# Seven half products for eight over 16 of the 22 down projection tiles of a decoder's feed-forward stage, with the residual kept in DRAM

## The chip, the cores and the metric

The kernel runs on one core of one Trainium2 chip. The metric is the time of one execution on the device in microseconds (us); each kernel is run several times and the median counts.

## The reference

One inference step of a one-layer hybrid decoder: 512 prompt tokens and 64 sample tokens (576 rows), model width 1024, feed-forward width 2816. Three recurrent branches come first and do not change here. The change lies in the last two lines:

```python
hf = rmsnorm(x, p["norm_pre_ffn"][l])
f = (jax.nn.silu(hf @ p["ffn_w_gate"][l]) * (hf @ p["ffn_w_up"][l])) @ p["ffn_w_down"][l]
x = x + rmsnorm(f, p["norm_post_ffn"][l])
```

Everything is float32.

## The kernel before

Activations lie transposed: features on the 128 partitions, tokens along the row, in two halves of NH = 288 tokens. The width 1024 is KT = 8 tiles, 2816 is FT = 22 tiles. A float32 product is made of three products of a reduced type (fp32r): each operand is split into a high part and a low remainder, and TensorE does high by high, high by low and low by high. So one 128x128 weight block against one half of the tokens is three matmuls of 128x288.

**Weights.** A load on SyncE (SP) brings a raw weight tile (`wr`) into SBUF. `wsplit` (L190) makes the high part `wh` on ScalarE (L198) and the low part `wl` = raw - high on VectorE (L199), 128x512 each. `wsplit_dma` (L178) makes the low part without VectorE: ScalarE copies the high part (L181) and its negative into the low part's buffer (L182), and a DMA issued by GpSimd (L183, a row `POOL DMA` in the trace) adds the raw weight from DRAM onto it. Buffers of `wh` and `wl` come from `ff_alloc` (L1434), which takes two pools of four in turn: a weight takes the buffer of the weight made eight before it, and its first copy waits until TensorE has read that one for the last time.

**Gate and up.** The first NG = 4 of 22 tiles are plain products. For the other 18 tiles, two at a time, `pair` (L1470) computes a 2x2 block product (two tiles of outputs by two halves of tokens) in seven half products for eight, in a Winograd form: seven weights, each against one of seven prepared activations `hx`, 12 matmuls per product, 84 instead of 96. `pair_w` (L1438) prepares the seven weights: four VectorE sums of raw quarters (L1448, L1449, L1450, L1455), four weights through `wsplit`, and three (numbers 0, 1 and 6) through `wsplit_dma`. Its work is issued under `tc.high_priority`, so the scheduler, which writes out the order of every engine's queue when the kernel is built, puts it between the products of the tiles ahead. Products run in the order 0, 2, 3, 4, 1, 5, 6, and VectorE combines them from PSUM by adds of 128x288.

**Down.** After the gate pair of every second step, `down(k0, 4)` (L1499) multiplies four finished tiles of the gated activations (`fh`, `fl`, made by `act_split`) by the down weights: for eight output tiles and two halves a full product of 12 matmuls each, 192 per chunk; weights through `wsplit` alone; the result is added to `mx` by VectorE (L1515), 16 adds of 128x288 per chunk. This is done for K tiles 0 to 15 in four chunks; `down(16, 2)` adds two more, and the last chunk of four tiles (L1541 on) is done half by half with the square, the norm and the output behind it. `mx` is the buffer `xr`; the residual `x1` stays in SBUF throughout.

## Time and profile before

| | us |
|---|---|
| median of 3 runs | 1097.94 (1096.48 to 1100.03) |
| the profiled execution, own time | 1097.48 |
| its span in the profile | 1095.6 |
| PE busy (7658 records) | 1036.4 (95%) |
| PEld busy | 989.7 (90%) |
| DVE busy | 779.4 (71%) |
| ACT busy | 508.2 (46%) |
| POOL busy | 164.4 (15%) |
| TensorE clock, mean over the span | 0.97 |
| the stage of feed-forward pairs and down chunks | about 705 to 1077 |

Busy is the union of an engine's instructions. PE is TensorE's matmuls, PEld its weight loads (one ahead of each matmul, beside the one before), DVE is VectorE, ACT ScalarE, POOL GpSimd; SPq is SyncE's queue of DMA issues. The reader should take the busy shares by stage, since the stages ahead of 705 us do not change.

### The profile page before, as it was taken

The numbers are of one execution on the slowest core, as the hardware profiler recorded it, in microseconds if no ns is written. First come the engines' busy times: TensorE is split into PE (matmuls) and PEld (weight loads), VectorE is DVE, ScalarE is ACT, GpSimd is POOL, SyncE is SP. The second block draws the span as 40 slices with busy tenths as digits, with TensorE's granted clock in tenths as the row PEclk, the third lists the DMA queues.
The fourth block names the chain that finished last, engine by engine and source line by source line (L and its number), as shares of the span: only waits on it lengthen the run. The fifth ranks groups of instructions, "written<-read, shape, count | busy, mean of one in ns | idle before, by whom it ended". The sixth has DMA issues, their size and how long they took to land.

```text
span 1095.6 us, 20107 instructions
## 1 busy us (share of the span) xinstructions
PE 1036.4 (95%) x7658; PEld 989.7 (90%) x7658; DVE 779.4 (71%) x1893; ACT 508.2 (46%) x1041; POOL 164.4 (15%) x224
## 2 busy tenths in 40 slices
PE   8889997799999999999799999899999999999994
PEld 6788896799999989998699999899999999999994
DVE  7978878737897769854637647874685766757756
ACT  5359667336444523332233445354653635635620
POOL 1132311110001210011000031200211201112124
PEclk9989997799999999999799999999999999999997
DMA  6656753373323134222112622134573736646502
GB/s 210 170 118 134 167 112 94 74 177 106 111 81 93 49 118 138 68 71 97 39 54 69 240 78 76 41 92 129 121 197 72 174 107 137 180 96 143 156 1 86
DMA packets 75139, 122.58 MB, mean 112 GB/s; under 512 B 28187, under 2 KB 36643, under 8 KB 75043
## 3 DMA queue, kind: packets, MB, share of 16 engines
q1 hardware_dynamic: 61938, 97.44, 27.6%
q0 software_dynamic: 13104, 23.86, 13.2%
q8 instruction: 60, 0.98, 0.4%
q14 instruction: 37, 0.30, 0.1%
HBM read 113.03 MB, written 8.24 MB: 111 GB/s over the span
## 4 chain that ended last, share of the span: by engine, by line
PE 74%; DVE 9%; DMA 7%; ACT 5%; issue 4%; POOL 1%; SPq 0%; DVEq 0%; POOLq 0%; ACTq 0%
PE mm L216 12%; PE mm L217 12%; PE mm L218 12%; PE mm L1466 9%; PE mm L1464 9%; PE mm L1465 9%; DMA wl<-in_w_in 1%; DVE wl L199 1%; DMA wl<-in_w_up 1%; ACT wh L181 1%; PE kp L1032 1%; DMA wr<-in_w_in 1%; DMA ys<-s5y 1%; PE zq L1203 1%; DMA wr<-in_w_gate 1%
## 5 line engine op out<-in xcount | busy, mean ns | idle before, releaser
L218 PE MATMUL mm<-hh,wl 128*128 128x288 f32 x768 | 231.3, 303 | 5.5 <-DMA wl<-in_w_in 5.5
L216 PE MATMUL mm<-hh,wh 128*128 128x288 f32 x768 | 231.4, 303 | 4.7 <-DVE u L412 2.4
L217 PE MATMUL mm<-hl,wh 128*128 128x288 f32 x768 | 231.6, 302 | 0.0
L198 ACT ACTIVATE wh<-wr 128x512 fp32r<-128x512 f32 x213 | 131.9, 629 | 212.4 <-PE mm L217 117.5
L199 DVE TENSOR_TENSOR wl<-wr,wh 128x512 fp32r<-128x512 f32 x213 | 146.8, 696 | 67.4 <-ACT wh L198 61.9
L216 PEld LDWEIGHTS mm<-hh,wh 128*128 128x128 f32 x768 | 145.8, 190 | 10.8 <-issue 5.8
L218 PEld LDWEIGHTS mm<-hh,wl 128*128 128x128 f32 x768 | 146.1, 191 | 8.6 <-DMA wl<-in_w_in 6.5
L217 PEld LDWEIGHTS mm<-hl,wh 128*128 128x128 f32 x768 | 146.1, 190 | 3.3 <-issue 2.9
L1466 PE MATMUL mm<-fh,wl 128*128 128x288 f32 x352 | 103.8, 295 | 0.0
L1464 PE MATMUL mm<-fh,wh 128*128 128x288 f32 x320 | 94.7, 296 | 0.0
L1465 PE MATMUL mm<-fl,wh 128*128 128x288 f32 x320 | 94.3, 295 | 0.0
L181 ACT ACTIVATE wh<-wr 128x512 fp32r<-128x512 f32 x91 | 56.8, 627 | 64.5 <-PE mm L1465 46.5
L1466 PE MATMUL mm<-hfh,wl 128*128 128x288 f32 x288 | 84.7, 296 | 1.0 <-DMA wl<-in_w_gate 0.8
L1465 PE MATMUL mm<-hfl,wh 128*128 128x288 f32 x288 | 84.9, 295 | 0.0
L1464 PE MATMUL mm<-hfh,wh 128*128 128x288 f32 x288 | 84.8, 295 | 0.0
L216 PE MATMUL mm<-brh,wh 128*128 128x288 f32 x224 | 67.4, 307 | 5.8 <-ACT brh L253 4.2
L217 PE MATMUL mm<-brl,wh 128*128 128x288 f32 x224 | 68.2, 306 | 0.2 <-DVE brl L254 0.2
L218 PE MATMUL mm<-brh,wl 128*128 128x288 f32 x224 | 67.5, 302 | 0.0
L1466 PEld LDWEIGHTS mm<-fh,wl 128*128 128x128 f32 x352 | 66.1, 188 | 0.0
L1465 PE MATMUL mm<-t,wh 128*128 128x288 f32 x216 | 63.9, 296 | 0.0
L1466 PE MATMUL mm<-t,wl 128*128 128x288 f32 x216 | 63.8, 295 | 0.0
L1464 PE MATMUL mm<-t,wh 128*128 128x288 f32 x216 | 63.7, 295 | 0.0
(506 smaller groups left out, 2580.8 us busy)
## 6 DMA issues: line engine op xcount, KB each, us to landing
wr<-in_w_in SPq DMA_DIRECT2D x48, 512.0 KB, 3.5
wr<-in_w_gate SPq DMA_DIRECT2D x22, 512.0 KB, 3.5
wr<-in_w_up SPq DMA_DIRECT2D x22, 512.0 KB, 3.5
wr<-in_w_down SPq DMA_DIRECT2D x20, 512.0 KB, 4.8
wl<-in_w_in POOLq DMA_DIRECT2D x30, 256.0 KB, 5.9
wl<-in_w_gate POOLq DMA_DIRECT2D x27, 256.0 KB, 4.5
wl<-in_w_up POOLq DMA_DIRECT2D x27, 256.0 KB, 4.4
wr<-in_w_out SPq DMA_DIRECT2D x8, 512.0 KB, 3.5
```

Of the source, the lines that this page charges most:

```text
L181: S.activation(hi, raw, AF.Copy)
L198: S.activation(hi, raw, AF.Copy)
L199: (eng or lo_eng()).tensor_tensor(lo, raw, hi.bitcast(F32), op=OP.subtract)
L216: PE.matmul(acc, hi[:, k, :], xh[:, sl], start=k0 + k == 0, stop=False)
L217: PE.matmul(acc, hi[:, k, :], xl[:, sl], start=False, stop=False)
L218: PE.matmul(acc, lo[:, k, :], xh[:, sl], start=False, stop=k0 + k == n - 1)
L1032: PE.matmul(kp[:, b], k2[:, sl], kqe[:, :, sl], start=True, stop=True)
L1203: PE.matmul(zqv[:, b], s0[:, b, :], kqe[:, :, c0:c0 + 8], start=True, stop=True)
L1464: PE.matmul(acc, hi[:, k0 + k, :], xh, start=new and k == 0, stop=False, skip_group_check=not new)
L1465: PE.matmul(acc, hi[:, k0 + k, :], xl, start=False, stop=False, skip_group_check=not new)
L1466: PE.matmul(acc, lo[:, k0 + k, :], xh, start=False, stop=k == len(x) - 1, skip_group_check=not new)
```

## The change

The down projection of K tiles 0 to 15 takes the same form as gate and up. Per chunk of four K tiles, `down7(k0)` treats four output pairs (two groups `g` by two pairs `e`) as 2x2 block products with two K tiles per side: seven half products of 6 matmuls per output pair, 168 per chunk. Two calls of `pair_w` per chunk make its weights, and each weight serves two output pairs, `e` = 0 and 1; so each chunk has 14 prepared weights, six of them through `wsplit_dma`. The activations need seven sides, made by `down_x0` and `down_x1`: four VectorE sums and seven splits of 128x2x288 per chunk. `down7` now stands after the up pair.

The term `u`, which the Winograd form adds to three of four quarters, is gathered over all chunks in `ut` and added to `mx` once at the end (four adds of 128x864). Accumulators add PSUM to SBUF: 28 adds of 128x288 per chunk (in the first chunk some are ScalarE copies). The buffer for `ut`, `pair`'s intermediates and one activation buffer is `fa`, a tile that `x1` lived in; `x1` is therefore stored to DRAM (`x1d`) before the stage and loaded again near its end. The last chunk has NL = 6 tiles instead of 4 after a chunk of 2: 18 matmuls per output tile and half. The host packs the down weights in two arrays.

```diff
+NL = 6
+    x1d = dr.tile([128, KT, NT], F32, name="x1d")
         rows = norm_rows(tq, ss, 1.0 / D, EPS)
+        SY.dma_start(x1d[:, :, sl], x1t[:, :, sl])
...
-            if half:
-                act_split(m)
     wqx.close()
+    fp = ctx.enter_context(tc.tile_pool(name="fp", bufs=7, reuse_waits="tile"))
...
+    fa = acc_tile("fa")
+    acts[2] = fa[:, 2:4, :]
...
+    def down_x0(k0):
+        t = act2(k0)
+        b11, b12 = (t[:, :, hsl(b)] for b in range(2))
+        dx[0] = fparts(b11)
+        V.tensor_tensor(b11, b12, b11, op=OP.subtract)
+        dx[3] = fparts(b11)
+
+    def down_x1(k0):
+        b11, b12, b21, b22 = quarters(k0)
+        V.tensor_tensor(b12, b22, b12, op=OP.subtract)
+        dx[4] = fparts(b12)
+        dx[5] = fparts(b22)
+        V.tensor_tensor(b22, b22, b11, op=OP.subtract)
+        dx[2] = fparts(b22)
+        dx[1] = fparts(b21)
+        V.tensor_tensor(b21, b21, b22, op=OP.subtract)
+        dx[6] = fparts(b21)
...
+    def down7(k0):
+        c = k0 == 0
+        for g in range(2):
+            ws = pair_w(i["w_down7"], k0 + 2 * g)
+            for e in range(2):
+                p_ = 2 * g + e
+                q = 2 * e
+                u = ut[:, p_, :]
+                c1, c2 = mx[2 * p_], mx[2 * p_ + 1]
+                px = product(ws[0], q, dx[0])
+                add_to(u, px, c)
+                V.tensor_tensor(u, u, product(ws[2], q, dx[2]), op=OP.add)
+                pz = product(ws[3], q, dx[3])
+                add_to(c2[:, hsl(1)], pz, c)
+                pw_ = product(ws[4], q, dx[4])
+                V.tensor_tensor(c2[:, hsl(1)], c2[:, hsl(1)], pw_, op=OP.add)
+                product(ws[1], q, dx[1], px)
+                add_to(c1[:, hsl(0)], px, c)
+                product(ws[5], q, dx[5], pz)
+                add_to(c1[:, hsl(1)], pz, c)
+                product(ws[6], q, dx[6], pw_)
+                add_to(c2[:, hsl(0)], pw_, c)
+
+    down_x0(0)
     for m in range(NG, FT, 2):
         t = act2(m)
         pair(i["w_gate"], m, lambda a, sl, c: glu_g(t[:, a, sl], c))
-        if m % 4 == 0 and m < FT - 2:
-            down(m - 4, 4)
+        k0 = m - 4 if m % 4 == 0 and m <= FT - NL else None
+        if k0 is not None:
+            down_x1(k0)
         pair(i["w_up"], m, lambda a, sl, c: glu_u(t[:, a, sl], c))
-        act_split(m)
-        act_split(m + 1)
-    down(FT - 6, 2)
+        if k0 is not None:
+            down7(k0)
+        if m >= FT - NL:
+            act_split(m)
+            act_split(m + 1)
+        elif m % 4 == 0:
+            down_x0(m)
+    for p_ in range(KT // 2):
+        v = mxt[:, 2 * p_:2 * p_ + 2, :].rearrange("p m n -> p (m n)")[:, NH:].rearrange("p (a n) -> p a n", n=NH)
+        V.tensor_tensor(v, v, ut[:, p_, None, :].to_broadcast([128, 3, NH]), op=OP.add)
...
+    x1 = [T("x1")[:, :NT] for _ in range(KT)]
+    for m in range(KT):
+        SY.dma_start(x1[m], x1d[:, m, :])
...
-                ps = product(wl_[m], 0, [(h_[:, sl], l_[:, sl]) for h_, l_ in fl])
+                xs = [(h_[:, sl], l_[:, sl]) for h_, l_ in fl]
+                wm = wl_[m // 4 * 3:m // 4 * 3 + 3]
+                ps = product(wm[m % 4 // 2][m % 2], 0, xs[:4], more=True)
+                product(wm[2][m % 4 // 2], 2 * (m % 2), xs[4:], ps, go=True)
```

TensorE's queue where a weight's buffer is freed and the next one to use it is wanted. In the kernel before, at the end of a gate pair: the low part `wl_12219` (weight 0 of the up pair behind it) takes the buffer of `wl_11957`, eight weights earlier, whose last reading is the second row. The left-out rows are 49 matmuls of the gate pair.

```order
L1465 MATMUL mm_12006<-hfl_7411,wh_11956 128x288
L1466 MATMUL mm_12006<-hfh_7410,wl_11957 128x288
L1466 MATMUL mm_12113<-hfh_7406,wl_12076 128x288
...
L1464 MATMUL mm_12256<-hfh_7404,wh_12218 128x288
L1465 MATMUL mm_12256<-hfl_7405,wh_12218 128x288
L1464 MATMUL mm_12270<-t_1450_8425,wh_12226 128x288
L1465 MATMUL mm_12270<-t_1451_8426,wh_12226 128x288
L1464 MATMUL mm_12284<-t_1452_8429,wh_12230 128x288
L1466 MATMUL mm_12256<-hfh_7404,wl_12219 128x288
```

Between the last reading of `wl_11957` and the first of `wl_12219` stand 55 matmuls; it is the shortest such distance in the queue of the kernel before.

The same of the changed kernel, behind the `down7` of the second chunk: the low part `wl_10299` (weight 0 of an up pair) takes the buffer of `wl_10034`, weight 6 of the second group of `down7`, whose second output pair is the second row here.

```order
L1471 MATMUL mm_10115<-fl_9712,wh_10033 128x288
L1472 MATMUL mm_10115<-fh_9711,wl_10034 128x288
L1472 MATMUL mm_10221<-t_1452_8429,wl_10171 128x288
L1470 MATMUL mm_10235<-t_1462_8652,wh_10174 128x288
...
L1470 MATMUL mm_10333<-hfh_7404,wh_10298 128x288
L1471 MATMUL mm_10333<-hfl_7405,wh_10298 128x288
L1470 MATMUL mm_10347<-t_1450_8425,wh_10306 128x288
L1471 MATMUL mm_10347<-t_1451_8426,wh_10306 128x288
L1472 MATMUL mm_10333<-hfh_7404,wl_10299 128x288
```

Here 17 matmuls stand between the two (11 of them left out).

VectorE's queue in the second down chunk. Before (`xr` is `mx`, `mm` a PSUM tile, `wl` a low part, L1455 a sum of `pair_w` for the next pair):

```order
L1515 TENSOR_TENSOR xr<-xr,mm_9745 128x288
L1515 TENSOR_TENSOR xr<-xr,mm_9759 128x288
L199 TENSOR_TENSOR wl_9951<-ws_9937,wh_9950 128x512
L1515 TENSOR_TENSOR xr<-xr,mm_9773 128x288
L1515 TENSOR_TENSOR xr<-xr,mm_9787 128x288
L199 TENSOR_TENSOR wl_9955<-wr_9935,wh_9954 128x512
L1515 TENSOR_TENSOR xr<-xr,mm_9811 128x288
L1515 TENSOR_TENSOR xr<-xr,mm_9825 128x288
L1455 TENSOR_TENSOR wr_9933<-wr_9933 128x512
```

After, at the end of the same chunk's `down7` (`fa` holds `ut`; L255 and L1521 are splits and a sum of the next chunk's activations, L1454 and L1460 sums of `pair_w`):

```order
L255 TENSOR_TENSOR fl_10145<-ar_8208,fh_10144 128x576
L200 TENSOR_TENSOR wl_10167<-wr_10153,wh_10166 128x512
L1454 TENSOR_TENSOR wr_10295<-wr_10293,wr_10295 128x512
L1552 TENSOR_TENSOR fa<-fa,mm_10099 128x288
L200 TENSOR_TENSOR wl_10171<-ws_10157,wh_10170 128x512
L1539 TENSOR_TENSOR xr<-xr,mm_10107 128x288
L1521 TENSOR_TENSOR ar_8208<-ar_8208 128x2x288
L200 TENSOR_TENSOR wl_10175<-wr_10155,wh_10174 128x512
L1460 TENSOR_TENSOR wr_10153<-wr_10153 128x512
L1539 TENSOR_TENSOR xr<-xr,mm_10091 128x288
```

Between the adds now stand the sums of `pair_w` for the next pair and the sums and splits of activations, which before were one split per pair.

## Rows read from the trace of the kernel before

**Rows 1.** Windows: us; busy (count) of PE, PEld, DVE, ACT, POOL; clock; DMA share; GB/s.
```profile
740.00:800.00 60.00, 60.00 (x454) 60.00 (x453) 34.95 (x63) 34.99 (x69) 9.02 (x11) 1.00 0.53 136
880.00:940.00 60.00, 60.00 (x454) 60.00 (x454) 41.18 (x78) 29.58 (x52) 8.86 (x11) 1.00 0.52 124
1000.00:1060.00 60.00, 59.72 (x445) 59.01 (x445) 43.26 (x87) 28.47 (x53) 9.26 (x11) 1.00 0.42 106
```

**Rows 2.** Waits of PEld from 740 to 1060: us, times, longest.
```profile
PEld mm L1466 <- DMA wl<-in_w_up: 0.6, 2, 0.3
PEld mm L1466 <- DMA wl<-in_w_gate: 0.5, 1, 0.5
```

**Rows 3.** Timeline of PE near its end: start, duration, instruction.
```profile
1071.33 0.30 PE L1466 MATMUL mm<-fh,wl 128*128 128x288 f32 x1
...
1076.92 0.29 PE L1466 MATMUL mm<-fh,wl 128*128 128x288 f32 x1
```

**Rows 4.** Lines of DVE by form, 795 to 1000: count, busy, mean ns, idle before.
```profile
L199 DVE TENSOR_TENSOR wl<-wr,wh 128x512 fp32r<-128x512 f32 x58 | 39.7, 689 | 5.0 <-ACT wh L198 3.3
L1515 DVE TENSOR_TENSOR xr<-xr,mm 128x288 f32<-128x288 f32 x48 | 21.7, 453 | 26.9 <-PE mm L1466 26.9
```

**Rows 5.** Timeline of DVE while it runs without a gap.
```profile
855.98 0.75 DVE L254 TENSOR_TENSOR fl<-ar,fh 128x576 fp32r<-128x576 f32 x1
856.65 0.45 DVE L1478 TENSOR_TENSOR cu<-cu,mm 128x288 f32<-128x288 f32 x1
857.02 0.68 DVE L199 TENSOR_TENSOR wl<-wr,wh 128x512 fp32r<-128x512 f32 x1
857.62 0.68 DVE L1449 TENSOR_TENSOR wr<-wr,wr 128x512 f32<-128x512 f32 x1
```

**Rows 6.** The page's group of L181's copies over the whole span.
```profile
L181 ACT ACTIVATE wh<-wr 128x512 fp32r<-128x512 f32 x91 | 56.8, 627 | 64.5 <-PE mm L1465 46.5
```

**Rows 7.** Timeline of ACT: starts of L181 at four weights.
```profile
970.02 0.63 ACT L181 ACTIVATE wh<-wr 128x512 fp32r<-128x512 f32 x1 [2.54 <-PE mm L1465]
...
990.95 0.62 ACT L181 ACTIVATE wh<-wr 128x512 fp32r<-128x512 f32 x1
...
1004.35 0.62 ACT L181 ACTIVATE wh<-wr 128x512 fp32r<-128x512 f32 x1
...
1016.41 0.62 ACT L181 ACTIVATE wh<-wr 128x512 fp32r<-128x512 f32 x1
```

**Rows 8.** Timeline of POOL: the accumulating DMAs of the first and third of these.
```profile
971.61 0.86 POOL L183 DMA_DIRECT2D wl<-in_w_up  x1 [11.78 <-DVE wr L1455]
...
1006.84 0.86 POOL L183 DMA_DIRECT2D wl<-in_w_gate  x1 [1.56 <-DVE ar L1396]
```

**Rows 9.** Timeline of PEld: the three loads that waited for a low part.
```profile
999.17 0.19 PEld L1466 LDWEIGHTS mm<-hfh,wl 128*128 128x128 f32 x1 [0.33 <-DMA wl<-in_w_up]
...
1011.60 0.19 PEld L1466 LDWEIGHTS mm<-hfh,wl 128*128 128x128 f32 x1 [0.45 <-DMA wl<-in_w_gate]
...
1022.78 0.19 PEld L1466 LDWEIGHTS mm<-hfh,wl 128*128 128x128 f32 x1 [0.29 <-DMA wl<-in_w_up]
```

**Rows 10.** Tile wl on POOL, 740 to 1040, 51 accumulating DMAs.
```profile
DMA to landing us min/median/max: 3.9/4.5/7.5
```

**Rows 11.** Timeline of DVE at the end of the last chunk.
```profile
1075.66 0.46 DVE L1547 TENSOR_TENSOR xr<-xr,mm 128x288 f32<-128x288 f32 x1 [0.53 <-PE mm L1466]
...
1078.72 0.44 DVE L1547 TENSOR_TENSOR xr<-xr,mm 128x288 f32<-128x288 f32 x1
```

**Rows 12.** Windows of 2 us around 706, where TensorE stood idle.
```profile
704.00:706.00 2.00, 0.82 (x3) 0.72 (x4) 2.00 (x6) 1.23 (x3) 0.00 (x0) 0.81 0.00 0
706.00:708.00 2.00, 2.00 (x10) 2.00 (x10) 2.00 (x4) 0.84 (x1) 0.00 (x0) 0.50 0.00 0
708.00:710.00 2.00, 2.00 (x15) 2.00 (x14) 2.00 (x5) 0.33 (x1) 0.00 (x0) 0.84 0.00 0
710.00:712.00 2.00, 2.00 (x17) 2.00 (x17) 2.00 (x3) 0.00 (x0) 0.00 (x0) 1.00 0.03 8
```

**Rows 13.** Waits of SyncE's queue, 600 to 1096.
```profile
SPq L1442 <- PE mm L218: 28.6, 1, 28.6
```

More of the change, by code (lines that the diff above doesn't have):

```diff
@@ L1386, in act2 @@
     def act2(m):
-        if m not in acts:
-            acts[m] = ar.tile([128, 2, NT], F32, name=nm("ar"), tag="ar")
-        return acts[m]
+        j = m // 2 % 3
+        if j not in acts:
+            acts[j] = ar.tile([128, 2, NT], F32, name=nm("ar"), tag=f"ar{j}")
+        return acts[j]
     def act(m):
@@ L1456, in pair_w, with product @@
         return [w0, w1, w2, w3, w4, wsplit(a12, ff_alloc, eng=V), wsplit_dma(a22, d22, ff_alloc)]
-    def product(w, k0, x, acc=None):
+    def product(w, k0, x, acc=None, more=False, go=False):
         hi, lo, _ = w
         new = acc is None
+        skip = not new and not go
         if new:
@@ L1463, in product @@
         for k, (xh, xl) in enumerate(x):
-            PE.matmul(acc, hi[:, k0 + k, :], xh, start=new and k == 0, stop=False, skip_group_check=not new)
-            PE.matmul(acc, hi[:, k0 + k, :], xl, start=False, stop=False, skip_group_check=not new)
-            PE.matmul(acc, lo[:, k0 + k, :], xh, start=False, stop=k == len(x) - 1, skip_group_check=not new)
+            PE.matmul(acc, hi[:, k0 + k, :], xh, start=new and k == 0, stop=False, skip_group_check=skip)
+            PE.matmul(acc, hi[:, k0 + k, :], xl, start=False, stop=False, skip_group_check=skip)
+            PE.matmul(acc, lo[:, k0 + k, :], xh, start=False, stop=k == len(x) - 1 and not more,
+                      skip_group_check=skip)
         return acc
+    prn = [0]
     def pair(src, m, f):
         ws = pair_w(src, m)
-        u = sx.tile([128, NH], F32, name=nm("cu"), tag="cu")
-        c12 = sx.tile([128, NH], F32, name=nm("c1"), tag="c1")
-        c2 = sx.tile([128, NT], F32, name=nm("c2"), tag="c2")
+        prn[0] ^= 1
+        u, c12 = fa[:, 4, hsl(prn[0])], fa[:, 5, hsl(prn[0])]
+        c2 = fa[:, 6 + prn[0], :]
         c21, c22 = c2[:, hsl(0)], c2[:, hsl(1)]
@@ L1490, in pair @@
         f(1, slice(0, NT), c2)
-    def down_w(m, k0, n):
-        raw = ff_raw()[:, 0:2 * n, :]
-        SY.dma_start(raw.rearrange("p (m k) c -> p m k c", m=2),
-                     i["w_down"][m:m + 2, :, k0:k0 + n, :].rearrange("m p k c -> p m k c"))
-        return raw
-    def down(k0, n):
-        for m in range(0, KT, 2):
-            raw = down_w(m, k0, n)
-            if n == 4:
-                ws = [(wsplit(raw[:, 4 * a:4 * a + 4, :], ff_alloc, eng=V), 0) for a in range(2)]
-            else:
-                w = wsplit(raw, ff_alloc, eng=V)
-                ws = [(w, n * a) for a in range(2)]
-            for a, (w, k_) in enumerate(ws):
-                for half in range(2):
-                    sl = hsl(half)
-                    ps = product(w, k_, [(fs_[k0 + k][0][:, sl], fs_[k0 + k][1][:, sl]) for k in range(n)])
-                    xv = mx[m + a][:, sl]
-                    if k0 == 0:
-                        S.activation(xv, ps, AF.Copy)
-                    else:
-                        V.tensor_tensor(xv, xv, ps, op=OP.add)
+    ut = fa[:, 0:2, :].rearrange("p a (b n) -> p (a b) n", n=NH)
@@ new lines, in fparts, with quarters @@
+    def fparts(src):
+        hi, lo = (fp.tile([128, 2, NH], F32R, name=nm(t), tag=t) for t in ("fh", "fl"))
+        split(src, hi, lo)
+        return [(hi[:, k, :], lo[:, k, :]) for k in range(2)]
+    dx = {}
+    def quarters(k0):
+        return [act2(k0 + 2 * a)[:, :, hsl(b)] for a in range(2) for b in range(2)]
+    def down_x0(k0):
[4 more added lines that the diff above has]
+        dx[3] = fparts(b11)
@@ new lines, in down_x1, with add_to @@
+    def down_x1(k0):
[8 more added lines that the diff above has]
+        dx[6] = fparts(b21)
+    def add_to(dst, ps, first):
+        if first:
+            S.activation(dst, ps, AF.Copy)
+        else:
+            V.tensor_tensor(dst, dst, ps, op=OP.add)
@@ L1593, in pack @@
     wd = kt(g["ffn_w_down"][0])
-    out["w_down"] = cc(wd)
+    out["w_down"] = cc(wd[:, :, FT - NL:, :])
+    w7 = wd[:, :, :FT - NL, :].reshape(2, 2, 2, 128, (FT - NL) // 4, 2, 2, 128)
+    out["w_down7"] = cc(w7.transpose(4, 0, 2, 3, 5, 1, 6, 7).reshape(FT - NL, 128, 8, 128))
     rw = np.zeros((4, 2, 128, 128), f)
```

21 lines of the change are left out of this document (12 added, 9 removed).

## The prediction

> **What bounds the kernel now.** I read the windows by stage first. From 740 us on TensorE is busy all the time: 60.00 of 60 us in two stretches of pairs and down chunks, 59.72 in a later one, while VectorE is busy for 35 to 43 of 60 us and ScalarE for 28 to 35 [rows 1]. Here the reader should see that one engine is full and the others have room. The waits say the same: in 320 us weight loads waited for three low parts, 1.1 us in all [rows 2]. So in this stage a matmul less is time less, as long as the others keep up. Its price is the pace, not the recorded duration (records overlap): from the start at 1071.33 to the start at 1076.92 it is 42 steps in 5.59 us, 0.1331 us each [rows 3]; 454 matmuls in 60 us give 0.132 [rows 1]. I take 0.133.
>
> Then I looked for what is nearest to becoming late. Three things feed TensorE: VectorE's sums and low parts, ScalarE's copies, and the accumulating DMAs. ScalarE's copies L181 stood idle for 64.5 us before they could start, 46.5 of it until a matmul L1465 was done [rows 6]: they wait until a buffer is free. So the DMA path starts when TensorE lets go of a buffer, and from there a chain runs whose length TensorE must cover with other matmuls.
>
> **What the change removes.** Four chunks of 192 matmuls become four of 168: 96 fewer. The two-tile chunk and the last four tiles (96 + 192 = 288 matmuls) become one chunk of six (8 tiles x 2 halves x 18 = 288): nothing. In the written-out order TensorE's queue is shorter by exactly 96 rows. 96 x 0.133 = **12.8 us less**.
>
> **What it adds on VectorE.** Back to back a 128x512 costs 0.60 us, a 128x576 0.67 and a 128x288 0.37, from start to start [rows 5]. In the kernel before a chunk cost 8 low parts x 0.60 + 16 adds x 0.37, 10.7 us (both kinds, 48 adds for three chunks, in [rows 4]). Now: 16 operations of `pair_w` (two calls of four sums and four low parts) x 0.60 = 9.6, 28 adds x 0.37 = 10.4, and 11 operations of 576 columns on the activations (four sums, seven low parts) x 0.67 = 7.4, together 27.4. A pair costs 8 x 0.60 + 5 x 0.37 + 1.4 for the gating = 8.05 us; a chunk's four pairs 32.2. So VectorE has 59.6 us to do in the (4 x 84 + 168) x 0.133 = 67 us of a chunk: 89%. It fits on average. Locally it does not: up pair, `down_x1`, `down7` and the next `down_x0` are 8.05 + 27.4 = 35.4 us of VectorE beside (84 + 168) x 0.133 = 33.5 us of TensorE. The lag of 1.9 us is taken up in the following gate, up and gate (24 of 33.5 us). I take nothing for it, since products stand in PSUM and prepared weights ahead of TensorE; if that cover is gone it costs 4 x 1.9 = 7.6 us.
>
> **What it adds on the DMA path: the term that decides.** Before, a down chunk had eight weights made by VectorE alone. Now it has 14 through `pair_w`, six of them with a low part by GpSimd's DMA: 74 such low parts in the stage instead of 51 (those of [rows 10]). Moreover each weight of `down7` is used twice, for `e` = 0 and 1, so its buffer is held over two output pairs and freed late, while the weight that takes it (eight later) is wanted soon. I counted in the order, for every such low part, the matmuls between the last reading of its buffer's former tenant and its own first reading. Before, the shortest are 55, 55 and four of 62; all others are 77 or more. After, 16 of 74 are under 49: 17, 26, 26, 32, 33, 33, 35, 35, 38, 38, 42, 43, 44, 44, 44, 47 (sum 577; the 17 and the 55 are the two excerpts of TensorE's queue).
>
> The chain that these must cover: from ScalarE's first copy, which starts when the buffer is free, to GpSimd's issue (970.02 to 971.61: 1.59 us; 1004.35 to 1006.84: 2.49) [rows 7, 8], and then to landing, at least 3.9, in the median 4.5, at most 7.5 us [rows 10]. So 5.5 at best, 6.1 in the median, 9.1 at worst. The three times that TensorE did wait tell the whole chain: from the copies at 990.95, 1004.35 and 1016.41 [rows 7] to the loads at 999.17, 1011.60 and 1022.78 [rows 9] 8.2, 7.3 and 6.4 us, mean 7.3. These are the late ones of 51. 55 matmuls cover 7.3 us, which is why before loses almost nothing; 17 cover 2.3 us.
>
> I take 6.5 us, nearer to the median chain than to the mean of the late ones, since many short leads take what the typical transfer gives. The shortfall of a low part is the chain less its lead: 16 x 6.5 - 577 x 0.133 = 104.0 - 76.7 = 27.3 us; where two short leads lie in one stretch one wait serves both, which takes off 1.7: **25.6 us more**. By the same sum a chain of 5.5 gives 13.4 (the ten leads up to 38, sum 313), 6.0 about 19, 7.0 about 33, 7.5 about 43. For the kernel before 7.5 gives 0.3, against 1.1 of waits seen [rows 2], so the method does not invent waits.
>
> The landing itself is what [rows 10] has. The Trainium skill, "DMA: Bandwidth & Descriptors", section "Anatomy of one DMA - SWDGE (gpsimd) path", puts such a DMA at 2.0 us plus its bytes over 436e3 per us; for the 256 KB of a low part that would be an estimate of 2.6 us, a chain of 4.2, a shortfall of some 3 us and a time of about 1087. This case's trace disagrees: its shortest landing is 3.9 and its median 4.5 us, so the measurement decides.
>
> **What else moves.** The store of `x1` stands on SyncE's queue ahead of loads which before waited 28.6 us for a matmul [rows 13]: hidden; if not, it is two transfers. Its reload stands ahead of the last chunk's 288 matmuls (38 us), and the residual is first used after half of them: hidden. The four adds of `ut` (128x864) fall while the last chunk's first products run. At the very end VectorE now lags: the last add of PSUM starts at 1078.72, 1.6 us after TensorE's last matmul ended (1077.2), behind adds of squares [rows 3, 11]. With 18 matmuls per tile instead of 12 it gets 0.8 us more per tile, so some of the 1.6 goes: between 0 and 1.6, I take **0.7 less**.
>
> **The sum**, against the profiled execution of 1097.48 us (span 1095.6; the median of the runs is 1097.94, 0.04% above): 1097.5 - 12.8 + 25.6 - 0.7 = 1109.6, so **1110 us**.
>
> **The rivals.**
> (a) *The gain holds, since the leads do not bind.* The scheduler's order says where a low part is read, and TensorE's weight loads might have enough else to do; or the landings are shorter than in the rows (a chain of 4.2 to 4.5: 3.4 to 4.7 us lost). 1097.5 - 13.5 + (0 to 4.7) = 1084 to 1089. Against it: 2.3 us of cover stands against a chain whose shortest observed form is 5.5. For it: the rows of TensorE's waits are only three. Chance 0.10.
> (b) *VectorE becomes the bound instead*, with the leads mostly covered because TensorE is late anyway: 7.6 us given back, 1097.5 - 13.5 + 7.6 = about 1092. For it: 35.4 against 33.5 us in each chunk. Against: average load of 89%. Chance 0.07.
> (c) *Break-even*: the chain is at its shortest everywhere (5.5), 13.4 lost against 13.5 won: about 1097. Here lies the point from which the sign turns: with a chain above 5.5 the kernel is slower, below it faster. Chance 0.14.
> (d) *Worse than forecast*: the chain is as long as the late ones (7.5, 43 us lost: 1127), or the clock falls in the waits. Of this the rows show one case: TensorE was idle for most of 704 to 706, then the granted clock was 0.50, the lower of its two levels (1.2 against 2.4 GHz), for the next 2 us, and 10 and 15 matmuls ran in two windows that later hold 17 [rows 12]. That is some 9 matmuls, 1.2 us; five such falls would cost 6. Chance 0.09.
> (e) *The change does not do what it says*: the 96 matmuls are gone from the queue, so I give it nothing.
>
> **How the numbers follow.** The forecast's own case, chains of 6.0 to 7.5, is 1103 to 1126 us with chance 0.60; (a) 0.10, (b) 0.07, (c) 0.14, (d) 0.09. A measurement of this kernel can tell about 0.3%, 3.3 us, from no change. Faster by more than that: (a) and (b), 0.17; within it: (c), 0.14; slower: the forecast and (d), 0.60 + 0.09 = 0.69. The range must leave out no more than 0.2: it drops (a) and (d), 0.19, and so goes from just under (b), 1091, to the top of the forecast, 1126.
>
> **What the profile after would show.** Right: weight loads of TensorE at the low-part matmul of `product` waiting for DMA, not 1.1 but some 25 us in all, in some ten to sixteen places, 2 to 4 us each, most at the first product of the pair after a `down7` and inside `down7`; the chain from copy to load at 6 to 7 us; TensorE busy for some 56 of 60 us. VectorE at 85 to 90% in the chunks. (a) would show TensorE full as before; (b) waits of TensorE, or of ScalarE, for VectorE's low parts or sums; (d) low-clock windows after waits. The forecast is wrong above all if accumulating DMAs land faster when issued at other times than in the rows, or if ScalarE starts its copies earlier than the release that I counted from, which would mean that buffers are not taken eight weights later.

## The result, and the profile after

The changed kernel takes 1110.14 us in the median of four runs (1104.77 to 1113.82) beside 1097.21 for the kernel before on the same chip: a ratio of 1.011 with a 95% interval of 1.0077 to 1.0143. It is slower by about 13 us, as forecast (1110). The profiled execution has a span of 1111.9 us against 1095.6; it is the slowest of the four and has the lowest mean clock (0.961, the others 0.967 to 0.971), so the clock's share in the sum below may be smaller in the median.

The page of the changed kernel, busy time and count of each engine: TensorE has the 96 matmuls less (7562 records for 7658), yet is busy longer, and every other engine has more to do.

```profile
PE 1039.3 (93%) x7562; PEld 987.1 (89%) x7562; DVE 823.1 (74%) x1985; ACT 539.5 (49%) x1105; POOL 184.5 (17%) x248
```

The windows that answer to [rows 1], columns as there:

```profile
740.00:800.00 60.00, 59.52 (x445) 58.73 (x444) 49.40 (x90) 45.45 (x93) 13.80 (x16) 1.00 0.72 170
880.00:940.00 60.00, 53.54 (x370) 52.88 (x369) 48.99 (x97) 31.32 (x56) 10.99 (x13) 0.91 0.59 127
1000.00:1060.00 60.00, 58.08 (x430) 56.93 (x429) 49.67 (x93) 37.42 (x67) 10.38 (x12) 1.00 0.72 177
```

Where 454 matmuls ran in 60 us, now 370 to 445 do. VectorE went from 35 to 43 us of 60 up to 49 to 50; the clock was 0.91 in one stretch that had 1.00.

Waits of TensorE's weight loads from 720 to 1095 us in the changed kernel (total, times, longest), which answer to [rows 2]:

```profile
PEld mm L1472 <- DMA wl<-in_w_down: 10.8, 8, 3.9
PEld mm L1472 <- DMA wl<-in_w_up: 5.8, 6, 2.9
PEld mm L1472 <- DMA wl<-in_w_gate: 4.6, 5, 1.5
PEld mm L1470 <- DVE fa L1489: 1.2, 3, 0.6
PEld mm L1470 <- ACT fa L1486: 1.1, 2, 0.7
```

Weight loads waited 21.2 us in 19 places for low parts that a DMA adds up; before it was 1.1 us in three. For VectorE and ScalarE they waited about 3 us. Only three of the 19 waits lasted 2 us or more, where the prediction had expected 2 to 4 us each. The landing time of these DMAs, of the low parts from 740 to 1060 us, is longer than in [rows 10] in the median (5.2 for 4.5):

```profile
DMA to landing us min/median/max: 3.9/5.2/7.9
```

The longest of the waits, followed back through three timelines of the changed kernel. ScalarE's copy started when TensorE had let go of the buffer, GpSimd issued 1.59 us later, and the load went 8.05 us after the copy:

```profile
918.49 0.64 ACT L182 ACTIVATE wh<-wr 128x512 fp32r<-128x512 f32 x1 [1.57 <-PE mm L1471]
```
```profile
920.08 0.86 POOL L184 DMA_DIRECT2D wl<-in_w_down  x1 [6.36 <-DVE xr L1539]
```
```profile
926.54 0.29 PEld L1472 LDWEIGHTS mm<-fh,wl 128*128 128x128 f32 x1 [3.94 <-DMA wl<-in_w_down]
```

What stands behind such a wait is seen in windows of 2 us, columns as in [rows 1], around the three longest:

```profile
840.00:842.00 2.00, 2.00 (x10) 2.00 (x10) 2.00 (x5) 0.59 (x1) 0.00 (x0) 0.50 0.01 1
842.00:844.00 2.00, 2.00 (x13) 2.00 (x12) 1.25 (x3) 1.16 (x3) 0.00 (x0) 0.68 0.00 0
...
894.00:896.00 2.00, 2.00 (x13) 2.00 (x11) 2.00 (x5) 0.48 (x1) 0.00 (x0) 0.62 0.14 24
896.00:898.00 2.00, 2.00 (x10) 2.00 (x10) 1.08 (x3) 2.00 (x6) 0.74 (x1) 0.53 0.43 90
...
924.00:926.00 2.00, 0.00 (x0) 0.00 (x0) 0.00 (x0) 0.00 (x0) 0.00 (x0) 0.80 0.99 242
926.00:928.00 2.00, 1.46 (x6) 1.46 (x7) 0.10 (x1) 0.00 (x0) 0.00 (x0) 0.50 1.01 298
928.00:930.00 2.00, 2.00 (x10) 2.00 (x9) 1.98 (x5) 0.86 (x2) 0.00 (x0) 0.50 0.14 57
930.00:932.00 2.00, 2.00 (x11) 2.00 (x10) 1.41 (x3) 1.08 (x2) 0.86 (x1) 0.50 0.00 0
```

TensorE is busy there and does 10 or 11 matmuls in 2 us where it otherwise does 17: the clock has fallen to its lower level (0.50) after the wait. In these windows 11, 11 and 19 matmuls are missing (6 in 1.46 us stand for 12), 41 x 0.133 = 5.5 us. The fall at the start of the stage, [rows 12], was longer too: 10, 10 and 12 matmuls in three windows, 19 missing instead of 9, 1.3 us more.

The end: TensorE's last product and the last add of PSUM.

```profile
1096.02 0.29 PE L1472 MATMUL mm<-fh,wl 128*128 128x288 f32 x1
```
```profile
1096.35 0.46 DVE L1614 TENSOR_TENSOR xr<-xr,mm 128x288 f32<-128x288 f32 x1 [0.45 <-PE mm L1472]
```

The last add now starts 0.04 us after TensorE's end (1096.31), not 1.5 us after it as in [rows 3, 11] (the prediction has 1.6). From TensorE's end to the span's end it is 15.6 us for 18.4.

**The sum of what was seen**, profiled execution against profiled execution: 96 matmuls -12.8; waits for low parts 21.2 - 1.9 = +19.3 (1.9 from 700 us on, of which 1.1 after 740); waits for VectorE and ScalarE +3; clock 5.5 + 1.3 = +6.8; the first matmul of the feed-forward stage 1.7 us later (673.59 for 671.88; the other kernels with the same code ahead of it lie between 669.7 and 674.3); the end -2.8. Together +15.2, where the spans differ by 16.3; 1 us is not placed. This is the bookkeeping of one execution against another; the experiments ask which of the terms can be taken away.

### The profile page after: what moved, and what is told of

Same layout as the page of the kernel before. It is cut to its first block, busy times and chain, and to the rows that moved or that the text cites. A ratio compares the mean times of both kernels' runs of the same rounds, so it can differ in the third digit from the quotient of the medians.

```text
span 1111.9 us, 20159 instructions
## 1 busy us (share of the span) xinstructions
PE 1039.3 (93%) x7562; PEld 987.1 (89%) x7562; DVE 823.1 (74%) x1985; ACT 539.5 (49%) x1105; POOL 184.5 (17%) x248
## 4 chain that ended last, share of the span: by engine, by line
PE 63%; DMA 11%; issue 11%; DVE 9%; ACT 3%; POOL 2%; SPq 0%; DVEq 0%; POOLq 0%; ACTq 0%
PE mm L217 13%; PE mm L219 12%; PE mm L218 12%; PE mm L1472 5%; PE mm L1470 5%; PE mm L1471 4%; DMA wl<-in_w_up 2%; DMA wl<-in_w_gate 2%; POOL wl L184 2%; DMA wl<-in_w_in 2%; DVE wl L200 1%; PE mm L408 1%; DMA wr<-in_w_gate 1%; DMA ys<-s5y 1%; PE kp L1033 1%
## 5 line engine op out<-in xcount | busy, mean ns | idle before, releaser
L199 ACT ACTIVATE wh<-wr 128x512 fp32r<-128x512 f32 x205 | 125.4, 627 | 172.9 <-PE mm L218 117.8
L200 DVE TENSOR_TENSOR wl<-wr,wh 128x512 fp32r<-128x512 f32 x205 | 141.2, 696 | 60.9 <-ACT wh L199 57.2
L182 ACT ACTIVATE wh<-wr 128x512 fp32r<-128x512 f32 x115 | 71.9, 628 | 83.9 <-PE mm L1471 63.0
L1472 PE MATMUL mm<-fh,wl 128*128 128x288 f32 x320 | 94.7, 304 | 9.1 <-DMA wl<-in_w_down 9.0
L1471 PE MATMUL mm<-fl,wh 128*128 128x288 f32 x288 | 86.0, 302 | 0.0
L1470 PE MATMUL mm<-fh,wh 128*128 128x288 f32 x288 | 84.8, 301 | 0.4 <-DVE ar L1402 0.4
L183 ACT ACTIVATE wl<-wh 128x512 fp32r<-128x512 f32 x115 | 72.0, 627 | 2.0 <-ACT wh L182 0.4
L1472 PEld LDWEIGHTS mm<-fh,wl 128*128 128x128 f32 x320 | 61.0, 193 | 11.1 <-DMA wl<-in_w_down 10.8
L1470 PE MATMUL mm<-t,wh 128*128 128x288 f32 x216 | 63.6, 296 | 0.0
L1472 PEld LDWEIGHTS mm<-hfh,wl 128*128 128x128 f32 x288 | 54.3, 190 | 10.4 <-DMA wl<-in_w_up 5.8
```

Of the source, the lines that this page charges most:

```text
L182: S.activation(hi, raw, AF.Copy)
L183: S.activation(lo, hi.bitcast(F32), AF.Copy, scale=-1.0)
L199: S.activation(hi, raw, AF.Copy)
L200: (eng or lo_eng()).tensor_tensor(lo, raw, hi.bitcast(F32), op=OP.subtract)
L1470: PE.matmul(acc, hi[:, k0 + k, :], xh, start=new and k == 0, stop=False, skip_group_check=skip)
L1471: PE.matmul(acc, hi[:, k0 + k, :], xl, start=False, stop=False, skip_group_check=skip)
```

## The experiments

All kernels are compared with the kernel before on the same chip. Since the start of the feed-forward stage moves by some microseconds from build to build, the table gives for the profiled execution the start of its first matmul and the time from there to the end of the span, and the waits of weight loads for low parts from 700 us on. The medians are of all runs and the profiled executions come from several chips, so rows are best compared by their ratios; executions of one kernel differ by about 1% (1.8% in interleave_lag), so differences of some 5 us between profiled executions say little by themselves.

| kernel | median us | ratio to before, 95% interval | stage starts | from there to the end | waits for low parts by DMA |
|---|---|---|---|---|---|
| before | 1097.2 | | 671.9 | 423.7 | 1.9 |
| changed | 1110.1 | 1.011 (1.008 to 1.014) | 673.6 | 438.3 | 21.2 |
| full_products | 1105.5 | 1.007 (1.004 to 1.009) | 673.2 | 430.6 | 8.5 |
| full_early | 1095.6 | 0.999 (0.997 to 1.002) | 674.0 | 422.6 | 2.8 |
| queue_order | 1146.2 | 1.045 (1.041 to 1.049) | 670.2 | 476.2 | 11.4 |
| interleave | 1112.8 | 1.014 (1.010 to 1.017) | 674.3 | 439.3 | 18.8 |
| interleave_order | 1124.0 | 1.024 (1.020 to 1.028) | 672.2 | 451.4 | 0.8 |
| interleave_lag | 1125.4 | 1.023 (1.015 to 1.031) | 672.2 | 448.1 | 1.6 |
| interleave_lag_raw | 1119.8 | 1.020 (1.015 to 1.025) | 669.7 | 445.0 | 2.2 |
| strict_fewer_sums | 1103.7 | 1.006 (1.002 to 1.009) | 673.9 | 428.6 | 1.5 |
| down_low_by_vector | 1107.2 | 1.010 (1.006 to 1.013) | 672.3 | 431.5 | 10.3 |
| negative_first | 1100.1 | 1.005 (1.002 to 1.008) | 662.5 | 433.3 | 20.7 |
| low_by_vector_early | 1105.3 | 1.007 (1.005 to 1.010) | 662.1 | 441.6 | 10.6 |
| negative_first_early | 1107.9 | 1.010 (1.007 to 1.013) | 663.0 | 442.4 | 18.3 |

**Plain products in the changed kernel (full_products), and the same with the chunk at its old place (full_early).** The first takes the seven half products out of the down chunks, with the sums of activations and the adds of `ut` that belong to them (these deletions are left out below), and leaves the rest of the change:

```diff
     def down7(k0):
+        xq = [[fparts(q) for q in quarters(k0)[2 * a:2 * a + 2]] for a in range(2)]
         for g in range(2):
+            for a in range(2):
+                raw = ff_raw()
+                SY.dma_start(raw, i["w_down7"][k0 + 2 * g + a])
+                w = [wsplit(raw[:, 4 * b:4 * b + 4, :], ff_alloc, eng=V) for b in range(2)]
+                for e in range(2):
+                    for half in range(2):
+                        ps = product(w[0], 2 * e, xq[0][half], more=True)
+                        product(w[1], 2 * e, xq[1][half], ps, go=True)
+                        add_to(mx[4 * g + 2 * e + a][:, hsl(half)], ps, k0 == 0)
```

> The changed kernel with plain products in place of the seven half products in the down chunks: x1 in DRAM, the last chunk of six tiles, the buffers and the packed weights stay as changed; the down weights are split by VectorE as before (192 matmuls a chunk). Theory (the accumulating DMAs land too late for the short distances that the order leaves): 51 low parts by DMA, shortest distance 54 matmuls, so weight loads wait under 2 us for low parts, and the time is that of before less what the longer last chunk gives at the end, 1093 to 1098 us. Rival (the store and reload of x1, the last chunk or the buffer sharing cost the time): 1103 us or more.

It took 1105.5: the rival's side. Yet the waits are for low parts all the same, those of the up weights (weight loads, 740 to 1090 us):

```profile
PEld mm L1472 <- DMA wl<-in_w_up: 7.0, 5, 3.2
```

That pointed to the place of the chunk rather than to the store of `x1`: behind the up pair and not, as before, between gate and up. The longest of these waits (3.2 us, at 748.6) is in the first up pair, which now stands right behind the first gate pair. The second kernel moves the call there:

```diff
+        if k0 is not None:
+            down7(k0)
         pair(i["w_up"], m, lambda a, sl, c: glu_u(t[:, a, sl], c))
-        if k0 is not None:
-            down7(k0)
```

> As the run with plain products in the changed kernel, with one thing moved: the down chunk stands between the gate and the up pair of its step, as in the kernel before, instead of behind the up pair. The store and reload of x1, the last chunk of six tiles and the buffers are as changed. Theory (the later place of the chunk made the 7 us of that run, since its low parts waited 8.5 us at the up pair behind the chunk): waits for low parts under 4 us, 1093 to 1099 us. Rival (x1 in DRAM, the last chunk or the buffers cost it): 1102 us or more.

```profile
PEld mm L1472 <- DMA wl<-in_w_up: 1.1, 2, 0.7
```

1095.6 us, no different from before (0.997 to 1.002). That settles two things. `x1` in DRAM, the buffers and the last chunk of six tiles together cost nothing that shows (from TensorE's last product to the end it is 16.9 us for 18.4, so up to 1.5 us may be hidden by that). And the later place alone, with plain products, costs some 8 us: 430.6 for 422.6 us from the stage's start, and as much by the ratios. The forecast had not priced the place.

**TensorE's products in the order of the program (queue_order), the two output pairs of a weight side by side (interleave), and both (interleave_order).** The scheduler may slip a product ahead of others; the first of these binds each product behind the one before it:

```diff
+        with tc.issue_after(lastmm[0]) if lastmm[0] is not None else nullcontext():
             for k, (xh, xl) in enumerate(x):
...
+        lastmm[0] = mm.ins if ordered[0] else None
```

> The changed kernel with one thing more: TensorE's products of the pairs and down chunks are issued in the order in which the program writes them, none slipped ahead of another. Counted in its order, the shortest distance from a buffer's last reading to the first reading of the low part that takes it is 44 matmuls (5.9 us; eight of them, then 50 and 62), instead of 17. Theory: a chain of 6 to 7 us lacks about 1 us eight times, so waits for low parts of 2 to 8 us instead of 21, no fall of the clock in the chunks, 1084 to 1092 us. Rival 1 (VectorE is the bound): TensorE now waits for VectorE's sums and splits instead, 1095 to 1110 us. Rival 2 (the number of accumulating DMAs or their traffic is what costs): no change, 1105 to 1113 us.

The second computes weight by weight, for `e` = 0 and 1, with weight 1 prepared and used earlier:

```diff
-            for e in range(2):
...
-                px = product(ws[0], q, dx[0])
-                add_to(u, px, c)
-                V.tensor_tensor(u, u, product(ws[2], q, dx[2]), op=OP.add)
+            px = [product(ws[0], 2 * e, dx[0]) for e in range(2)]
+            for e in range(2):
+                add_to(us[e], px[e], c)
+            for e in range(2):
+                V.tensor_tensor(us[e], us[e], product(ws[2], 2 * e, dx[2]), op=OP.add)
...
```

> The changed kernel with the two output pairs of a down weight computed one right behind the other (weight 0 for both, weight 2 for both, 1, 3, 4, 5, 6), so that a buffer is not held over a whole output pair; the order is again left to the scheduler. Counted in its order the short distances remain (29, 32, 32, 33, 38, 38, 39, 40 and more, fifteen under 45), as the scheduler pulls the next pair's first products ahead. Theory (distance in the queue decides, whatever makes it short): waits for low parts of 10 to 20 us, 1097 to 1108 us. Rival (holding a weight over two output pairs is the cause): waits gone, 1082 to 1088 us.

> Both: the two output pairs of a down weight one right behind the other, and TensorE's products in the order of the program. The shortest distance is 86 matmuls, 11.5 us, more than the longest chain seen. The same 168 matmuls, 28 adds, 74 accumulating DMAs and VectorE sums as the change. Theory: no wait for a low part, the 12.8 us of the 96 matmuls come in full and the end is shorter, 1081 to 1086 us. Rival 1 (VectorE is the bound): waits for VectorE of 7 us or more, 1089 to 1100 us. Rival 2 (the accumulating DMAs cost by their number): 1100 us or more.

Weight-load waits of the three. queue_order:

```profile
PEld mm L1473 <- DVE fa L1493: 26.1, 12, 5.4
PEld mm L1475 <- DMA wl<-in_w_down: 10.5, 6, 2.1
PEld mm L1473 <- DVE xr L1560: 9.6, 7, 2.6
```

interleave:

```profile
PEld mm L1475 <- DMA wl<-in_w_down: 9.1, 5, 2.9
PEld mm L1475 <- DMA wl<-in_w_gate: 7.3, 7, 1.5
```

interleave_order:

```profile
PEld mm L1476 <- DVE fa L1496: 17.9, 10, 3.7
PEld mm L1476 <- ACT fh L254: 6.5, 2, 3.4
PEld mm L1476 <- DVE fa L1498: 4.9, 5, 1.2
```

All three times missed on the slow side (interleave by 5 us, the other two by far), and the rows say why. On low parts the expectation held, with distances as the expectations count them: with a shortest distance of 86 matmuls they waited 0.8 us in all, with 44 matmuls 11.4, with fifteen distances under 45 it was 18.8. The second rival to interleave_order has its time, 1100 us or more, but not its cause: all the accumulating DMAs of the change are there, land later than in the changed kernel (median 6.1 us for 5.2), and almost nothing waits for them. Whether a weight is held over two output pairs does not matter by itself: interleave alone, whose order the scheduler chose, has short distances again and is as slow as the change. But a product that adds to a PSUM tile must wait until VectorE has read that tile (L1493 and L1496 are the add `c22 = u + pz` of `pair`, L1498 the one behind it, L1560 an add of `down7`), and in program order nothing can slip past it. The waits for VectorE that take the place of the DMA's are 41 us in one kernel and 23 us in the other (with 6.5 for ScalarE's splits). The second rival of the prediction, VectorE, is real. It stayed hidden in the changed kernel, whose only difference from queue_order is that the scheduler may fill these waits with products pulled ahead; and the pulled products make distances short (29 matmuls in interleave, 86 with the same products in program order).

**Looser order (interleave_lag), a fifth raw buffer (interleave_lag_raw), fewer sums (strict_fewer_sums).**

```diff
-        with tc.issue_after(lastmm[0]) if lastmm[0] is not None else nullcontext():
+        with tc.issue_after(lastmm[-2]) if len(lastmm) >= 2 else nullcontext():
```

> As the run with the two output pairs interleaved and the products in program order, but looser: each product of TensorE is bound only to the one before the previous, so that the scheduler may slip one product past one other. The shortest distance counted in its order is 62 matmuls (8.3 us), on nearly all low parts 74 or more. Theory after the first runs (two holders: low parts by DMA where distances are short, VectorE's queue where TensorE may not slip): almost no waits for low parts, 0 to 2 us, and fewer waits for VectorE than the 30 us of the strict order, about 10 to 20: 1095 to 1110 us. Rival 1 (strictness alone made the waits for VectorE): waits under 5 us, 1082 to 1090 us. Rival 2 (VectorE holds whatever the order): 1118 us or more.

```diff
-        return (wp if rawn[0] % 2 else sx).tile([128, KT, 128], F32, name=nm("wr"), tag="wr", bufs=2)
+        j = rawn[0] % 5
+        return (wp if j in (1, 3) else sx).tile([128, KT, 128], F32, name=nm("wr"), tag="wr", bufs=2 if j in (1, 3) else 3)
```

> The same with a fifth buffer for raw weights, where four are taken in turn otherwise. In the runs so far VectorE's sums of a pair stood at the head of its queue until a raw weight had been loaded (in the strict interleaved order 45 us of such waits, in the changed kernel 26), and PSUM adds that TensorE needs stood behind them. Theory (VectorE is late by what stands at its queue's head, not by its amount of work): waits of VectorE for raw weights fall by a third or more, and the time is 3 to 10 us under the run without it. Rival (VectorE's amount of work holds): the same within 2 us.

```diff
-            V.tensor_tensor(s1, a21, a22, op=OP.add)
-            V.tensor_tensor(a21, a11, a21, op=OP.subtract)
-            V.tensor_tensor(a11, s1, a11, op=OP.subtract)
+            if sums:
+                V.tensor_tensor(s1, a21, a22, op=OP.add)
+                V.tensor_tensor(a21, a11, a21, op=OP.subtract)
+                V.tensor_tensor(a11, s1, a11, op=OP.subtract)
+            else:
+                s1 = a22
```

> The interleaved kernel in program order, with the four VectorE sums of weights left out in the down chunks (32 operations of 128x512, 19 us of VectorE in all; the down weights are then raw quarters, so that this part of the computation is not done). TensorE's order, its matmuls and the DMAs are the same. Theory (in program order TensorE waits for VectorE): waits for VectorE fall from some 30 us to under 15, and the time from 1124 to 1095 to 1110 us. Rival (it waits for something else that the records put down to VectorE, as a late DMA): 1118 us or more.

Slipping past one product does not help (1125.4, the side of the second rival; 16.7 us of waits for the same add). The fifth raw buffer gives 1119.8, with an interval that overlaps that of the kernel without it, and the expected cause did not show: VectorE's waits for raw weights in the two kernels (its sums from 720 to 1100 us; idle time before them behind the bar) are 49.5 us without and 45.4 with it.

```profile
L1453 DVE TENSOR_TENSOR ws<-wr 128x512 f32<-128x512 f32 x26 | 18.0, 692 | 31.9 <-DMA wr<-in_w_up 13.6 <-DMA wr<-in_w_gate 11.0 <-DMA wr<-in_w_down 7.2
L1454 DVE TENSOR_TENSOR wr<-wr,wr 128x512 f32<-128x512 f32 x26 | 17.9, 690 | 17.6 <-DMA wr<-in_w_gate 9.8 <-DMA wr<-in_w_down 4.7 <-DMA wr<-in_w_up 3.1
```
```profile
L1454 DVE TENSOR_TENSOR ws<-wr 128x512 f32<-128x512 f32 x26 | 18.0, 692 | 45.4 <-DMA wr<-in_w_gate 18.5 <-DMA wr<-in_w_down 15.4 <-DMA wr<-in_w_up 11.4
```

Taking 32 sums of 128x512 (19 us of VectorE) out of the strict interleaved kernel took 20 us off its time (1124.0 to 1103.7), as the theory expected, and the waits for that add fell from 17.9 to 4.1 (line 1501 there):

```profile
PEld mm L1481 <- ACT fh L254: 4.9, 2, 2.8
PEld mm L1481 <- DVE fa L1501: 4.1, 4, 1.7
```

In program order these sums are thus paid nearly one for one, though from 740 to 1060 us VectorE is busy for only 251 of 320 us in the strict interleaved kernel: it is late by stretches, not on average. The edit also shortens the way from a raw weight to its split, and no run tells the two apart. And even with neither the waits for low parts nor these sums, the kernel takes 428.6 us from the stage's start where the kernel before takes 423.7: it still waits for ScalarE's splits and VectorE's adds.

**Low parts of the down weights by VectorE (down_low_by_vector).**

```diff
+    def pair_w(src, m, dve=False):
...
-            w0 = wsplit_dma(a11, d11, ff_alloc)
+            w0 = wsplit(a11, ff_alloc, eng=V) if dve else wsplit_dma(a11, d11, ff_alloc)
...
-            ws = pair_w(i["w_down7"], k0 + 2 * g)
+            ws = pair_w(i["w_down7"], k0 + 2 * g, True)
```

> The changed kernel with all low parts of the down weights made by VectorE: 24 accumulating DMAs and 48 of ScalarE's copies fewer (24 come back as nothing), 24 VectorE operations of 128x512 more (14.4 us in all, 3.6 per chunk, which makes 63 of 67 us). Theory (two holders): the waits for low parts of down weights (10.8 us) go, those of gate and up stay at about 10, waits for VectorE rise by as much as was won: 1100 to 1115 us. Rival 1 (only the DMA path holds): 1094 to 1100 us. Rival 2 (VectorE's work holds): 1118 us or more.

```profile
PEld mm L1473 <- DMA wl<-in_w_up: 6.0, 5, 2.3
PEld mm L1473 <- DMA wl<-in_w_gate: 4.3, 4, 2.7
...
PEld mm L1471 <- ACT wh L199: 2.3, 5, 1.0
PEld mm L1471 <- DVE fa L1490: 2.0, 2, 1.4
```

As expected: the 10.8 us of waits for down weights are gone, the 10.4 us of gate and up weights stay at 10.3, and waits for VectorE and ScalarE rise by some 4 us. 1107.2 us; the median is 3 us under the change, within its spread.

**The negative first (negative_first), and two mixtures (low_by_vector_early, negative_first_early).**

```diff
-            S.activation(hi, raw, AF.Copy)
-            S.activation(lo, hi.bitcast(F32), AF.Copy, scale=-1.0)
+            S.activation(lo, raw, AF.Copy, scale=-1.0)
             G.dma_start(lo, src, accum_op=OP.add)
+            S.activation(hi, raw, AF.Copy)
```

> The changed kernel with ScalarE's two copies of a DMA's weight exchanged: the negative is made first, from the raw weight, and GpSimd's DMA starts behind it, so that the high part's copy (0.66 us) is off the chain. Nothing else is written otherwise; the scheduler's order changes with it (shortest distances 19, 26, 35, 37, 40, 41, 41, 44). Theory (chain against distance): the chain is 5.9 us instead of 6.5, and by the sum of shortfalls the waits for low parts fall from 21 to about 11 us: 1096 to 1104 us. Rival (the DMA's own time of landing, or its number, decides): within 3 us of the changed kernel, 1107 to 1113 us.

1100.1 us is inside the range expected, and for another reason than expected. Waits for low parts did not fall (720 to 1140 us):

```profile
PEld mm L1472 <- DMA wl<-in_w_down: 9.5, 6, 4.2
PEld mm L1472 <- DMA wl<-in_w_gate: 6.2, 6, 1.9
PEld mm L1472 <- DMA wl<-in_w_up: 5.0, 3, 2.9
```

ScalarE's timeline shows that the edit did not do what it was made for. In all 77 pairs of copies from 720 us on the high part (L184) is still copied ahead of the negative (L182), as the scheduler put it there; in the two examples the chain lost 0.14 us of 1.59 (964.81 to 965.33 between the two copies, where it was 918.49 to 919.15), not 0.66:

```profile
964.81 0.62 ACT L184 ACTIVATE wh<-wr 128x512 fp32r<-128x512 f32 x1
965.33 0.61 ACT L182 ACTIVATE wl<-wr 128x512 fp32r<-128x512 f32 x1
```

What got shorter lies ahead of the feed-forward stage, which uses the same helper: its first matmul is at 662.46 us instead of 673.59, and in the two mixtures, which share the edit, at 662.14 and 662.99.

```profile
662.46 0.42 PE L217 MATMUL mm<-hfh,wh 128*128 128x288 f32 x2
```

In the stage itself 438.3 became 433.3, which is within what single executions differ by. So this run says nothing against or for the chain. Most of the gain comes between 100 and 200 us, where TensorE does 687 matmuls for 632 in the changed kernel; its cause stays open.

> Three steps together on the changed kernel: low parts of the down weights by VectorE, the negative first for those of gate and up, and the down chunk between the gate and the up pair. Shortest distances 42, 48, 48, 49, 50. Theory: waits for low parts under 4 us; what is left are waits for VectorE (about 10 us in the run with low parts by VectorE) and a shorter end: 1088 to 1100 us. Rival (VectorE's work, 63 of 67 us of a chunk, holds the kernel as soon as the DMAs do not): 1103 us or more.

> The changed kernel with the negative copied first and with the seven half products of a down chunk between the gate and the up pair; the low parts of down weights stay with the DMA. Shortest distances 33, 43, 44, 44, 46, 46, 46, 48 against a chain of 5.9 us (44 matmuls). Theory: low parts wait 2 to 6 us where the run with the negative alone still waits about 10; 1090 to 1099 us, which would be the kernel before or a little under it. Rival (VectorE holds next, since its stretch of sums, splits and adds now stands before the up pair): 1102 us or more, with waits for VectorE of 10 us.

Both missed: 1105.3 and 1107.9 us although the stage starts 11 us earlier. From the stage's start they take 441.6 and 442.4, more than their relatives with the chunk behind the up pair (431.5 and 433.3). The waits of negative_first_early from 720 us on:

```profile
PEld mm L1472 <- DMA wl<-in_w_down: 11.1, 7, 2.9
PEld mm L1470 <- ACT fh L254: 6.9, 3, 2.3
PEld mm L1472 <- DMA wl<-in_w_up: 4.1, 5, 1.8
PEld mm L1470 <- DVE fa L1539: 3.3, 2, 2.3
```

With the chunk early, the splits of the activations (L254) that `down7` needs have no pair to hide behind: TensorE waits 6.9 us for them, and not at all in negative_first. The place that saves some 8 us with plain products costs 9 to 10 with the seven half products. And the sum of shortfalls, which gave 2 to 6 us here, was wrong again: 18.3 us of waits for low parts.

## Why the prediction was right, point by point

- **The time, 1110 for 1110.1 us.** Right, and in part by luck: errors in the distances, in the chain and in what was left out went against each other, as the next points show.
- **What bounds the kernel, and the 12.8 us.** Right as bookkeeping: 96 records fewer, and TensorE's waits and clock account for all but 1 us of the rest. No run got the 12.8 us back as time: where the waits for low parts are gone, others stand in their place.
- **Waits for low parts, +25.6.** Right in kind, place and nearly in size: 19.3 more, in 19 places. interleave_order shows that they are a matter of distance and not of the number of such DMAs: with all of them and long distances the waits are gone. Both factors of the size were wrong. The first is the list of distances. It assumed, as the section on the kernel before says too, that a weight takes the buffer of the weight eight before. Where it counted 17 matmuls, the shortest of all, ScalarE's copy began at 860.41, while the last reading of the supposed former tenant was loaded at 863.86:

```profile
859.23 0.19 PEld L1472 LDWEIGHTS mm<-t,wl 128*128 128x128 f32 x1
...
863.86 0.19 PEld L1472 LDWEIGHTS mm<-fh,wl 128*128 128x128 f32 x1
...
867.79 0.19 PEld L1472 LDWEIGHTS mm<-hfh,wl 128*128 128x128 f32 x1 [1.49 <-DMA wl<-in_w_up]
```
```profile
860.41 0.62 ACT L182 ACTIVATE wh<-wr 128x512 fp32r<-128x512 f32 x1
```
```profile
861.99 0.86 POOL L184 DMA_DIRECT2D wl<-in_w_up  x1 [0.84 <-ACT wl L183]
```

  The addresses of the buffers in the built program say the same: `wl_10299` lies where `wl_10167` lay, a low part of the gate pair, last read 52 matmuls before (the load at 859.23). The rule of eight fails for 22 of the 78 low parts that a DMA makes in this stage (before for 7 of 54, where the shortest distances are 38, 52, 55 and 55). By the addresses the distances under 49 are eleven, not sixteen: 26, 32, 38, 38, 38, 40, 42, 44, 44, 44, 46 (sum 432), and the forecast's chain of 6.5 us would have lost 11 x 6.5 - 432 x 0.133 = 14 us over them instead of 27.3.

  The second is the chain, which was longer than 6.5 us where it mattered. With TensorE's loads taken in the program's order, the 19 waits are all first readings of such low parts: seven at distances of 26 to 44 matmuls (8.8 us) and twelve at 49 to 67 (12.5 us), where 6.5 us would have cost nothing. From the load of the buffer's last reading to the load that waited it took 5.9 to 9.6 us, 8.2 in the median. In the rows above it is 8.56: 1.18 until ScalarE began its copy, between other work, 1.58 to GpSimd's issue, 5.80 to the load. So the list was too short in distance and the chain too short in time, and the two errors went against each other.

  With one chain of 7.0 us and the distances by address, the sum of shortfalls gives 21.6 us for the changed kernel (21.2 measured), 21.4 for interleave (18.8), 12.5 for queue_order (11.4), 1.9 for interleave_order (0.8) and 2.0 for the kernel before (1.9). It is too low by 3 to 6 us in negative_first (17.6 for 20.7), down_low_by_vector (7.0 for 10.3), low_by_vector_early (6.0 for 10.6), full_products (3.6 for 8.5) and negative_first_early (12.3 for 18.3). In negative_first, full_products and negative_first_early some 3 us of this is one wait for a low part whose buffer no earlier weight of the stage held, so that it has no distance at all. The 7.0 is fitted to the changed kernel. So the sum orders most of the kernels, but it is no tool for a forecast to a few microseconds.
- **The range.** Its top was taken too low: the sums for chains of 7.0 and 7.5 us (33 and 43) leave out the counted distances of 49 to 56, which the check against the kernel before does include (its 0.3 us come from distances of 55). With them the same list gives 37 and 49.
- **The cause given for short distances** (each weight of `down7` is used twice) was only part of it. interleave took it away and waited 18.8 us; it matters once the order is bound (44 matmuls in queue_order, 86 in interleave_order). The rest is the scheduler's slipping of products past late ones. The place of the chunk has a part too: full_products waits 8.5 us with plain products, full_early 2.8.
- **The clock.** Named in rival (d) with 1.2 us per fall, not in the sum. It fell three times in the chunks and cost 6.8 us with the fall at the start. The forecast's 25.6 came so near because it stood for 19.3 of waits, 3 of VectorE and part of this.
- **VectorE, taken as nothing.** Nearly right in the changed kernel (3 us; VectorE is busy for 263 of the 320 us from 740 to 1060, 82%), but its cover is the slipping (queue_order); in program order it costs 23 to 41 us, three to five times the 7.6 that rival (b) gave it.
- **The end, -0.7.** Under-sized: -2.8. The add's lag of 1.5 us went whole; the other 1.3 us lie in the norm and the output and were not traced.
- **The store and reload of `x1`, and the last chunk, taken as nothing.** Right within some 1.5 us: full_early.

The page of the Trainium skill ("DMA: Bandwidth & Descriptors", "Anatomy of one DMA - SWDGE (gpsimd) path") would have given a landing of 2.6 us as an estimate; in the changed kernel the median is 5.2 and the minimum 3.9. The measurement decides again.

None of the runs beats the kernel before. The kernel before with the negative copied first, to which the earlier start of the stage in three runs points, was not tried.

## What to carry to other kernels

When a schedule is already full, price a change by what the removed work was covering: here 12.8 us of matmuls were exchanged for chains of 6 to 10 us that the remaining matmuls no longer spanned, and for clock falls behind each long wait. Follow one late item through its whole chain (buffer free, copy, issue, landing, use), and verify, in the trace or by the addresses in the built program, which buffer it took before counting on a rotation. A time that comes out as expected proves nothing until the wait that should have gone is seen to be gone: negative_first gained its 10 us in another stage.

## What the runs showed of the hardware that was not expected

Waits of 2.1 to 3.9 us in an otherwise full TensorE were followed by 3 to 6 us at a granted clock of 0.50, so that the longest wait (3.94 us) cost a further 2.5 us (19 matmuls). Landing times of the accumulating DMAs grew from a median of 4.5 to 5.2 us as the DMA share in the chunks went from 0.42 to 0.53 up to 0.59 to 0.72; that the traffic lengthens them was not tested by itself.
